# A decoder layer on one core: convolution taps of six pairs moved from accumulating DMAs to VectorE, and a snapshot of begun products taken earlier

## The chip, the cores and the metric

The kernel runs on one core of a Trainium2 chip. The metric is the device time in microseconds (us), lower is better. TensorE is called PE, VectorE DVE, ScalarE ACT, GpSimd POOL and SyncE SP, as the profile does.

## What is computed

One layer of a network on 512 tokens of width 2048, batch 1, in float32: an input projection, a gated convolution beside dilated attention, an output projection, LayerNorm, and then the part around the change, a gated MLP of width 5632 with a causal convolution of width 3 between its two projections, and a second LayerNorm.

```python
def _causal_conv3(x, w):
    xp = jnp.pad(x, ((0, 0), (2, 0), (0, 0)))
    return w[0] * xp[:, :-2] + w[1] * xp[:, 1:-1] + w[2] * xp[:, 2:]

def _conv_ffn(h, w_up, conv_w, conv_b, w_down):
    up = _causal_conv3(h @ w_up, conv_w) + conv_b
    a, g = jnp.split(up, 2, axis=-1)
    return (jax.nn.silu(g) * a) @ w_down

def reference(x, ...):
    mix = _token_mixer(x, w_in, conv_w, w_out, rel_bias)     # conv mixer and attention
    x = _layernorm(ALPHA * x + mix, ln1_g, ln1_b)
    ffn = _conv_ffn(x, w_up, ffn_conv_w, ffn_conv_b, w_down)
    return _layernorm(ALPHA * x + ffn, ln2_g, ln2_b)
```

## The kernel before

**Order of the work.** Four stages follow each other: the input projection (48 pairs of column tiles, 0 to about 965 us), attention with the start of the output projection, the up projection (44 pairs, about 1265 to 2125 us), and the down projection. Each engine runs its own instructions strictly in the order in which the program issues them; nothing is scheduled by a planner. Work that must wait is put off with `later(n, fn)`: a list that `tick()` counts down by one after every product. Loads of weights go through SP's queue, stores and the accumulating transfers through POOL's.

**Pairs and products.** The two projections are computed by a Strassen-Winograd scheme: a pair of column tiles takes seven products, numbered 1 to 7, instead of eight. Each product accumulates into one half of a PSUM bank ("m" with the regions x1 and x2, "n" with x3 and x4). A later product adds to the same region, so between the two ACT must copy the region out; this copy is a snapshot (`snap`, L476, and L455 in wide pairs). Products 1, 5, 6 and 7 have one.

**Splits.** Weights are float32 and are multiplied in two parts. For each product DVE first forms a combination of the weight blocks if it needs one (T1 to T4, lines 207, 209, 211), ACT rounds it to `whi` (L221), DVE subtracts (`wlo`, L224). A ring of four such parts is filled ahead of PE: after a product is freed, the split of the product four places on is issued. So on ACT the snapshots stand between the `whi` of later products.

**Start of a projection.** While the inputs of later products are still being formed, `run_pre` begins one plain pair (pair 0) and products 1 and 2 of five further pairs (pairs 1 to 5). These five are finished afterwards by `run_pairs` with the remaining products `REST = [5, 6, 3, 7, 4]`; pairs from 6 on run all seven (`MAIN = [1, 5, 2, 6, 3, 7, 4]`) in `run_wide`. In a rest pair the order of the accumulations is: product 6 and then 7 go into x1, where product 1 is; product 3 goes into x3, where product 5 is. So snapshot 1 must be done before product 6 starts, snapshot 5 before product 3 and snapshot 6 before product 7.

**After a pair.** `combine` on DVE (L675) adds the banks and the snapshots to the pair's output `o`, first for bank m, then for n; n is combined after the first product of the next pair. Then `done3` makes the convolution and the gate: ACT writes the last tap and the bias to `cv` (L1130); for each of the other two taps ACT scales `o` (L1136) and a DMA on POOL's queue adds the shifted result to `cv` (L1137); seven ticks after `done3` for pairs 0 to 5, nine for later ones, ACT applies the silu to one half of `cv` (L1142), and one tick on DVE multiplies the halves (L1147) and a DMA stores them (`act_d`). For the last pair, 43, the taps are made on DVE instead (`taps`, two SCALAR_TENSOR_TENSOR of 128x511 and 128x510 for each half, L701), with no accumulating DMA:

```python
        def gate():
            if last:
                taps(cv[:, 1], o[:, 1], fw_t[:, j + FT])
            nc.scalar.activation(cv[:, 1], cv[:, 1], AF.Silu)
```

In the input projection `done1` uses the same `taps` for its pairs of kind c (after a multiplication on DVE, L710, and two scaled copies on ACT, L713), and a multiplication L717 closes a pair of kind b.

## Time and profile before

| | us |
|---|---|
| runs before, median of 3 (lowest, highest) | 2617.13 (2614.83, 2621.01) |
| the profiled execution's own time | 2616.42 |
| its span, first to last instruction | 2614.5 |
| PE, DVE, ACT, POOL busy in the span | 2572.5, 2109.6, 1317.6, 228.1 |

The profiled execution took 2616.42 us, 1.9 us more than its span. A busy PE is not yet a PE at its peak: the clock that the chip grants to TensorE is at full speed (2.4 GHz) or at half (1.2 GHz). In the rows "idle before <-releaser" is how long the engine waited before an instruction and what ended that wait.

### The profile page before, as it was taken

What the parts mean: (1) busy time and instruction counts of PE and PEld (TensorE: products, weight loads), DVE (VectorE), ACT (ScalarE), POOL (GpSimd) and SP (SyncE); (2) the same over time, 40 slices, a digit from 0 to 9 for tenths busy, and PEclk for the clock granted to TensorE, in tenths of its full rate; (3) what the DMA queues carried; (4) which work ended last, traced back from release to release, by engine and by line L of the source; (5) the groups of instructions that cost most, each with busy time, mean ns of one, the idle gap of its engine ahead of it and who ended that gap; (6) DMA issues with size and microseconds to landing.
All of it is one profiled execution on the core that took longest, in us unless ns stands there. A gap on an engine that the chain in (4) does not pass through costs nothing.

```text
span 2614.5 us, 36642 instructions
## 1 busy us (share of the span) xinstructions
PE 2572.5 (98%) x14634; PEld 2257.9 (86%) x14634; DVE 2109.6 (81%) x2553; ACT 1317.6 (50%) x1789; POOL 228.1 (9%) x301
## 2 busy tenths in 40 slices
PE   9999999999999999999989999999999999999997
PEld 8988888888888888888987888888888888888886
DVE  7889899899898887656868899889888866765557
ACT  5444444444444454435656676676676653222220
POOL 0000100000000012221011111111111110000000
PEclk9999999999999999999999999999999999999999
DMA  7333534334334367653566666667666683434331
GB/s 261 137 107 136 178 133 151 121 135 148 121 138 144 121 238 263 222 182 113 177 182 169 165 176 182 165 178 180 165 180 178 165 257 142 153 125 161 113 113 65
DMA packets 93610, 421.13 MB, mean 161 GB/s; under 512 B 11296, under 2 KB 37184, under 8 KB 58752
## 3 DMA queue, kind: packets, MB, share of 16 engines
q1 hardware_dynamic: 51968, 313.57, 34.9%
q0 software_dynamic: 41472, 105.22, 16.2%
q8 instruction: 115, 1.88, 0.3%
q14 instruction: 55, 0.45, 0.1%
HBM read 328.61 MB, written 48.84 MB: 144 GB/s over the span
## 4 chain that ended last, share of the span: by engine, by line
PE 88%; DVE 4%; DMA 3%; issue 2%; ACT 2%; SPq 0%; POOL 0%; DVEq 0%; ACTq 0%; POOLq 0%
PE bk L355 38%; PE bk L358 20%; PE bk L524 8%; PE bk L523 8%; PE bk L525 8%; PE bk L382 1%; PE bk L379 1%; PE bk L378 1%; DMA cv<-t 1%; DVE wlo L224 1%; ACT whi L221 1%; PE bk L856 1%; DMA cv<-o 1%; DMA ar<-act_d 1%; PE bk L802 1%
## 5 line engine op out<-in xcount | busy, mean ns | idle before, releaser
L221 ACT ACTIVATE whi<-raw 128x1024 fp32r<-128x1024 f32 x754 | 791.0, 1056 | 834.4 <-PE bk L525 223.5
L224 DVE TENSOR_TENSOR wlo<-raw,whi 128x1024 fp32r<-128x1024 f32 x754 | 919.7, 1221 | 170.4 <-ACT whi L221 157.7
L355 PE MATMUL bk<-S,whi 128*128 128x512 f32 x2560 | 643.2, 393 | 6.3 <-ACT z L455 6.1
L355 PEld LDWEIGHTS bk<-S,whi 128*128 128x128 f32 x2560 | 461.4, 189 | 89.6 <-ACT z L455 6.5
L355 PE MATMUL bk<-A,whi 128*128 128x512 f32 x1920 | 481.4, 393 | 0.0
L355 PEld LDWEIGHTS bk<-A,whi 128*128 128x128 f32 x1920 | 345.6, 189 | 63.3 <-issue 0.9
L358 PEld LDWEIGHTS bk<-S,wlo 128*128 128x128 f32 x2560 | 350.1, 191 | 25.1
L358 PE MATMUL bk<-S,wlo 128*128 128x256 f32 x2560 | 357.7, 283 | 0.0
L358 PEld LDWEIGHTS bk<-A,wlo 128*128 128x128 f32 x1920 | 261.9, 190 | 18.7
L358 PE MATMUL bk<-A,wlo 128*128 128x256 f32 x1920 | 267.7, 282 | 0.0
L524 PE MATMUL bk<-wlo,A 128*128 128x512 f32 x480 | 187.0, 389 | 1.6 <-DVE wlo L224 1.6
L525 PE MATMUL bk<-whi,A 128*128 128x512 f32 x480 | 186.7, 389 | 0.0
L523 PE MATMUL bk<-whi,A 128*128 128x512 f32 x480 | 186.7, 389 | 0.0
L436 DVE TENSOR_TENSOR z<-bk,z 128x512 f32<-128x512 f32 x152 | 104.2, 686 | 64.6 <-ACT z L433 64.6
L455 ACT ACTIVATE s<-bk 128x512 f32<-128x512 f32 x126 | 75.2, 597 | 129.6 <-PE bk L358 129.5
L1004 DVE TENSOR_TENSOR zz<-zz,bk 128x512 f32<-128x512 f32 x144 | 97.7, 687 | 32.9 <-PE bk L525 32.4
L455 ACT ACTIVATE z<-bk 128x512 f32<-128x512 f32 x114 | 67.3, 590 | 91.0 <-PE bk L358 91.0
L209 DVE TENSOR_TENSOR raw<-raw,raw 128x1024 f32<-128x1024 f32 x90 | 109.7, 1219 | 0.4
L211 DVE TENSOR_TENSOR raw<-raw,raw 128x1024 f32<-128x1024 f32 x90 | 109.8, 1220 | 0.0
L211 DVE TENSOR_TENSOR raw<-raw 128x1024 f32<-128x1024 f32 x90 | 109.8, 1220 | 0.0
L207 DVE TENSOR_TENSOR raw<-raw 128x1024 f32<-128x1024 f32 x90 | 109.7, 1218 | 0.0
L524 PEld LDWEIGHTS bk<-wlo,A 128*128 128x128 f32 x480 | 90.1, 188 | 20.8 <-DVE wlo L224 2.2
(216 smaller groups left out, 3406.8 us busy)
## 6 DMA issues: line engine op xcount, KB each, us to landing
raw<-in_w_in_dram SPq DMA_DIRECT2D x97, 1024.0 KB, 5.0
raw<-in_w_up_dram SPq DMA_DIRECT2D x89, 1024.0 KB, 7.5
raw<-in_w_down_dram SPq DMA_DIRECT2D x44, 1024.0 KB, 4.9
cv<-t POOLq DMA_DIRECT2D x43, 511.0 KB, 9.4
cv<-o POOLq DMA_DIRECT2D x43, 510.0 KB, 5.0
qkv_d<-o POOLq DMA_DIRECT2D x36, 512.0 KB, 3.1
raw<-in_w_out_dram SPq DMA_DIRECT2D x16, 1024.0 KB, 7.0
act_d<-cv POOLq DMA_DIRECT2D x44, 256.0 KB, 9.3
```

Source lines behind the costliest of these rows:

```text
L207: nc.vector.tensor_sub(b["T"], v[0], v[1])
L209: nc.vector.tensor_sub(b["T"], v[0], b["T"])
L211: nc.vector.tensor_sub(v[0], v[0], b["T"])
L221: nc.scalar.activation(self.hi, self.src, AF.Copy)
L224: nc.vector.tensor_sub(self.lo, self.src, self.hi.bitcast(F32))
L355: mm(ps, op.hi[:, w], X[xn].both(k), start=first and k == 0, stop=False, skip_group_check=True)
L358: mm(ps[:, 256:], op.lo[:, w], X[xn][0][:, k], start=False, stop=last and k == 7, skip_group_check=True)
L436: nc.vector.tensor_add(u, pairb[p][reg], u)
L455: nc.scalar.activation(sn[q], pairb[p][PROD[q][2]], AF.Copy)
L523: mm(banks[n], yh[:, tt], op.hi[:, w], start=first and i == 0, stop=False)
L524: mm(banks[n], yh[:, tt], op.lo[:, w], start=False, stop=False)
L525: mm(banks[n], yl[:, tt], op.hi[:, w], start=False, stop=last and i == 1)
```

## The change

For pairs 0 to 5 of the up projection the taps are made on DVE as for pair 43 (`last` holds for `j < 6`), with the silu one tick after the pair's combination and the product of the halves two ticks after it. And snapshot 1 of each rest pair, in both projections, is no longer taken when the pair begins: `prepare(p + 1)` takes it after product 3 of the pair before (for pair 1: after the second product of the plain pair), together with the allocation of the pair's two snapshot tiles.

```diff
-TAPS, TAPSPRE = 9, 7
+TAPS = 9
...
+    early = {}
+
+    def prepare(p, stile):
+        sn = early[p] = {b: stile(b).rearrange("p (a t) -> p a t", a=2) for b in "mn"}
+        b, i = SNAP[1]
+        nc.scalar.activation(sn[b][:, i], region(p, PROD[1][2]), AF.Copy)
+
-    def run_plain(pl, X, otile, done, hook):
+    def run_plain(pl, X, otile, done, hook, stile):
...
                 op = product(p, q, X, not _banks(q) & set().union(*map(_banks, seq[i + 1:])))
+                if i == 1 and p + 1 in [r for r, s, _ in pl if s == REST]:
+                    prepare(p + 1, stile)
...
-            sn = {b: stile(b).rearrange("p (a t) -> p a t", a=2) for b in "mn"}
+            sn = early.pop(p)
...
-            if 1 not in seq:
-                snap(1)
...
                 if q in SNAP:
                     snap(q)
+                if q == 3 and p + 1 in [r for r, s, _ in pl if s == REST]:
+                    prepare(p + 1, stile)
...
-        o, cv, last = fh(o), fh(cvtile()), j == FT - 1
+        o, cv, last = fh(o), fh(cvtile()), j == FT - 1 or j < sum(PRE3)
...
-        n = TAPSPRE if j < sum(PRE3) else TAPS
-        later(n, gate)
-        later(n + 1, mul)
+        later(TAPS, gate)
+        later(TAPS + 1, mul)
```

Lines move by 8 to 10: in the rows of the change L404 is `prepare`'s snapshot, L486 the other snapshots, L1140 the last tap with its bias, L1152 the silu, L711 the taps, L685 the combination, L1157 the product of the halves.

ACT in the up projection, from the silu of pair 0 to the last snapshot of pair 2 and the first of pair 3, before (bk_1624 is bank m of pair 2, bk_1719 its bank n, bk_1628 bank m of pair 3, where the second and third of its snapshots read):

```order
L1142 ACT_TABLE_LOAD
L1142 ACTIVATE cv_11835<-cv_11835 128x512
L1136 ACTIVATE t_12070<-o_11966,fw_t 128x512 x2
L476 ACTIVATE z_11969<-bk_1624_11166 128x256
L221 ACTIVATE whi_12099<-raw_11868 128x1024
L1136 ACTIVATE o_11966<-o_11966,fw_t 128x512 x2
L221 ACTIVATE whi_12133<-raw_11866 128x1024
L476 ACTIVATE z_12139<-bk_1628_11197 128x256
L476 ACTIVATE z_12139<-bk_1737_12142 128x256
L221 ACTIVATE whi_12169<-raw_11868 128x1024
L476 ACTIVATE z_12140<-bk_1628_11197 128x256
```

The same stretch of ACT in the change, from the last tap of pair 1 on:

```order
L1140 ACTIVATE cv_12003<-o_11969,fw_t 128x512 x2
L486 ACTIVATE z_11900<-bk_1624_11166 128x256
L221 ACTIVATE whi_12032<-raw_11868 128x1024
L1152 ACTIVATE cv_12003<-cv_12003 128x512
L404 ACTIVATE z_12067<-bk_1628_11197 128x256
L221 ACTIVATE whi_12072<-raw_11868 128x1024
L486 ACTIVATE z_11900<-bk_1624_11166 128x256
L221 ACTIVATE whi_12104<-raw_11870 128x1024
L221 ACTIVATE whi_12133<-raw_11868 128x1024
L486 ACTIVATE z_12067<-bk_1735_12139 128x256
L221 ACTIVATE whi_12166<-raw_11870 128x1024
```

The silu (there of pair 0, here of pair 1) no longer stands ahead of scaled taps; the copies L1136 are gone; snapshot 1 of pair 3 (from bk_1628) stands three products ahead of snapshot 5 (from bk_1735); the last tap L1140 stands between the `whi` and snapshot 6 of pair 2.

DVE over one rest pair of the up projection (raw is a weight block, wlo the low half of a split), before:

```order
L207 TENSOR_TENSOR raw_11866<-raw_11866 128x1024
L224 TENSOR_TENSOR wlo_11999<-raw_11671,whi_11998 128x1024
L224 TENSOR_TENSOR wlo_12031<-raw_11866,whi_12030 128x1024
L209 TENSOR_TENSOR raw_11866<-raw_11868,raw_11866 128x1024
L224 TENSOR_TENSOR wlo_12067<-raw_11866,whi_12066 128x1024
L1147 TENSOR_TENSOR cv_11835<-cv_11835 128x512
L211 TENSOR_TENSOR raw_11866<-raw_11866 128x1024
L224 TENSOR_TENSOR wlo_12100<-raw_11868,whi_12099 128x1024
L675 TENSOR_TENSOR o_12137<-bk_1624_11166,z_11968 128x2x256
L211 TENSOR_TENSOR raw_11868<-raw_11868,raw_11866 128x1024
L224 TENSOR_TENSOR wlo_12134<-raw_11866,whi_12133 128x1024
L675 TENSOR_TENSOR o_12137<-bk_1719_11971,z_11969 128x512
```

DVE over the same stretch in the change:

```order
L207 TENSOR_TENSOR raw_11868<-raw_11868 128x1024
L224 TENSOR_TENSOR wlo_11999<-raw_11671,whi_11998 128x1024
L711 SCALAR_TENSOR_TENSOR cv_12003<-o_11969,fw_t,cv_12003 128x511
L711 SCALAR_TENSOR_TENSOR cv_12003<-o_11969,fw_t,cv_12003 128x510
L224 TENSOR_TENSOR wlo_12033<-raw_11868,whi_12032 128x1024
L209 TENSOR_TENSOR raw_11868<-raw_11870,raw_11868 128x1024
L711 SCALAR_TENSOR_TENSOR cv_12003<-o_11969,fw_t,cv_12003 128x511
L711 SCALAR_TENSOR_TENSOR cv_12003<-o_11969,fw_t,cv_12003 128x510
L1157 TENSOR_TENSOR cv_12003<-cv_12003 128x512
L224 TENSOR_TENSOR wlo_12073<-raw_11868,whi_12072 128x1024
L211 TENSOR_TENSOR raw_11868<-raw_11868 128x1024
L224 TENSOR_TENSOR wlo_12105<-raw_11870,whi_12104 128x1024
```

Four taps now stand in each pair, two behind the split that follows T1 (L207) and two behind T2 (L209), and the multiplication of the halves, which was that of an earlier pair, follows its own taps. The last rows of the fence before, with the combinations L675, stand in the change behind those shown.

ACT at the start of the rest pairs of the input projection (sm and sn are snapshot tiles, bk_31_152 is bank m of pair 1 and bk_103_782 its bank n), before:

```order
L533 ACTIVATE S_94_663<-o_657 128x2x256
L221 ACTIVATE whi_719<-raw_434 128x1024
L221 ACTIVATE whi_746<-raw_477 128x1024
L221 ACTIVATE whi_775<-raw_434 128x1024
L476 ACTIVATE sm_779<-bk_31_152 128x256
L476 ACTIVATE sm_779<-bk_103_782 128x256
L221 ACTIVATE whi_809<-raw_477 128x1024
L402 ACTIVATE o_813<-bk_53_334 128x256
```

And in the change:

```order
L543 ACTIVATE S_94_663<-o_657 128x2x256
L404 ACTIVATE sm_717<-bk_31_152 128x256
L221 ACTIVATE whi_722<-raw_434 128x1024
L221 ACTIVATE whi_749<-raw_477 128x1024
L221 ACTIVATE whi_778<-raw_434 128x1024
L486 ACTIVATE sm_717<-bk_103_782 128x256
L221 ACTIVATE whi_809<-raw_477 128x1024
L410 ACTIVATE o_813<-bk_53_334 128x256
L410 ACTIVATE o_813<-bk_57_369 128x256
L486 ACTIVATE sn_718<-bk_31_152 128x256
```

Snapshot 1 has moved ahead of three `whi`, snapshot 5 stays behind them. Apart from these moves no engine has other instructions in another order: PE's and SP's sequences are the same, and POOL's loses the twelve accumulating transfers of pairs 0 to 5.

## Rows read from the trace of the kernel before

**Rows 1.** The page's first part: busy time, share of the span and number of instructions of each engine.

```profile
PE 2572.5 (98%) x14634; PEld 2257.9 (86%) x14634; DVE 2109.6 (81%) x2553; ACT 1317.6 (50%) x1789; POOL 228.1 (9%) x301
```

**Rows 2.** The waits of PE over the whole run, those at the rest pairs and behind them: who waited for whom, us in total, times, longest us.

```profile
PE bk L378 <- ACT z L476: 8.4, 3, 3.1
PE bk L355 <- ACT z L455: 6.1, 2, 3.1
PE bk L378 <- ACT sm L476: 3.5, 1, 3.5
```

**Rows 3.** PE in order of time, first matmuls of products: start us, duration us, engine, line, operation, tiles and shapes, count, in brackets the idle time before and its releaser. The first two are product 7 and product 4 of pair 2 of the up projection; then the stalled product 6 of pair 3, and that of pair 4 with the product that follows it; then the stalled product 7 of wide pair 7 and the three products that follow it; the last three rows are product 6 of pair 1 of the input projection, the product after it, and product 7 of pair 2 there.

```profile
1307.99 0.28 PE L378 MATMUL bk<-S,whi 128*128 128x256 f32 x1
1310.87 0.28 PE L378 MATMUL bk<-A,whi 128*128 128x256 f32 x1
...
1319.79 0.39 PE L378 MATMUL bk<-S,whi 128*128 128x256 f32 x1 [3.01 <-ACT z L476]
...
1337.60 0.39 PE L378 MATMUL bk<-S,whi 128*128 128x256 f32 x1 [3.14 <-ACT z L476]
...
1342.07 0.28 PE L378 MATMUL bk<-S,whi 128*128 128x256 f32 x1
...
1407.59 1.22 PE L355 MATMUL bk<-S,whi 128*128 128x512 f32 x2 [3.12 <-ACT z L455]
...
1412.88 0.94 PE L355 MATMUL bk<-A,whi 128*128 128x512 f32 x2
...
1416.00 2.00 PE L355 MATMUL bk<-A,whi 128*128 128x512 f32 x8
...
1418.79 0.63 PE L355 MATMUL bk<-S,whi 128*128 128x512 f32 x2
...
70.07 0.58 PE L378 MATMUL bk<-S,whi 128*128 128x256 f32 x1 [3.50 <-ACT sm L476]
...
75.36 0.37 PE L378 MATMUL bk<-S,whi 128*128 128x256 f32 x1
...
92.70 0.28 PE L378 MATMUL bk<-S,whi 128*128 128x256 f32 x1
```

**Rows 4.** Windows of some us: window and its length, busy us and count of PE, weight loads, DVE, ACT, POOL, then the granted clock (1.00 is 2.4 GHz, 0.50 is 1.2 GHz), the DMA share and GB/s.

```profile
70.00:75.00 5.00, 4.93 (x23) 4.93 (x24) 4.41 (x6) 1.89 (x5) 0.00 (x0) 0.50 0.43 121
1336.00:1342.00 6.00, 4.40 (x24) 4.41 (x25) 6.00 (x7) 2.87 (x5) 1.18 (x1) 0.72 0.92 201
...
1408.00:1414.00 6.00, 6.00 (x20) 5.05 (x20) 5.69 (x7) 3.72 (x5) 0.53 (x1) 0.54 0.96 297
```

**Rows 5.** The first row is the longest entry of the waits of ACT from 1280 to 1420 us, the second that of DVE's waits for the silu there; then ACT in order of time before the stall at 1319.79: the silu with its table load, and two snapshots of pair 3 (columns as in rows 3).

```profile
ACT cv L1142 <- DMA cv<-o: 18.3, 5, 6.6
...
DVE cv L1147 <- ACT cv L1142: 15.8, 5, 6.0
...
1312.94 1.28 ACT L1142 ACT_TABLE_LOAD   x1 [2.61 <-DMA cv<-o]
...
1319.38 0.64 ACT L476 ACTIVATE z<-bk 128x256 f32<-128x256 f32 x2
```

**Rows 6.** DVE in order of time: in the input projection the T1 of a pair, two of its four taps, the multiplication that closes a pair and the T1 of the next pair; in the up projection the T1 of pair 2, and a multiplication of halves of pair 43 behind its silu; last a row of the view of line 701, with the number and the least, median and longest duration in ns of pair 43's taps.

```profile
88.80 1.22 DVE L207 TENSOR_TENSOR raw<-raw 128x1024 f32<-128x1024 f32 x1
...
91.07 1.53 DVE L701 SCALAR_TENSOR_TENSOR o<-o,cw_t,o 128x511 f32<-128x511 f32 x2
...
103.35 1.22 DVE L717 TENSOR_TENSOR o<-o,o 128x1024 f32<-128x1024 f32 x1
104.49 1.22 DVE L207 TENSOR_TENSOR raw<-raw 128x1024 f32<-128x1024 f32 x1
...
1290.61 1.22 DVE L207 TENSOR_TENSOR raw<-raw 128x1024 f32<-128x1024 f32 x1
...
2135.32 0.69 DVE L1147 TENSOR_TENSOR cv<-cv 128x512 f32<-128x512 f32 x1 [3.22 <-ACT cv L1142]
...
L701 DVE SCALAR_TENSOR_TENSOR cv<-o,fw_t,cv x4: 745/751/752, 2130.6 to 2136.7; 128x511 f32<-128x511 f32 x2, 128x510 f32<-128x510 f32 x2
```

**Rows 7.** The links of a chain over two engines in order of time: on DVE the combination of bank n of pair 1 and the T1 behind it; on ACT a snapshot, and the two instructions of the last tap with the start of the next instruction.

```profile
1303.12 0.68 DVE L675 TENSOR_TENSOR o<-bk,z 128x512 f32<-128x512 f32 x1
1303.72 1.22 DVE L207 TENSOR_TENSOR raw<-raw 128x1024 f32<-128x1024 f32 x1
...
1359.13 0.38 ACT L476 ACTIVATE z<-bk 128x256 f32<-128x256 f32 x1 [1.58 <-PE bk L382]
...
1360.36 1.51 ACT L1130 ACTIVATE cv<-o,fw_t 128x512 f32<-128x512 f32 x2
1361.78 1.04 ACT L221 ACTIVATE whi<-raw 128x1024 fp32r<-128x1024 f32 x1
```

**Rows 8.** ACT and DVE in order of time in the input projection: the snapshots 1 and 5 of pair 1, DVE's wait behind the late product 6, and the scaled copies L713 with snapshot 6 of pair 2 behind them.

```profile
69.65 0.64 ACT L476 ACTIVATE sm<-bk 128x256 f32<-128x256 f32 x2
...
76.96 1.23 DVE L224 TENSOR_TENSOR wlo<-raw,whi 128x1024 fp32r<-128x1024 f32 x1 [1.36 <-ACT whi L221]
...
88.91 1.34 ACT L713 ACTIVATE o<-o,cw_t 128x512 f32<-128x512 f32 x2 [0.44 <-DVE o L710]
...
90.16 0.36 ACT L476 ACTIVATE sn<-bk 128x256 f32<-128x256 f32 x1
```

More of the change, by code (lines that the diff above doesn't have):

```diff
@@ L723, in done1 @@
             nc.gpsimd.dma_start(qkv_d[a:a + 2, :, slot, :].rearrange("h p t -> p h t"), o)
-    run_plain(plan1, X, otile1, done1, hook)
+    run_plain(plan1, X, otile1, done1, hook, stile1)
     run_pairs(plan1, X, stile1, otile1, bands1, done1, None, block1)
@@ L1157, in done3 @@
             later(1 + sh, functools.partial(tap, sh))
-        n = TAPSPRE if j < sum(PRE3) else TAPS
-        later(n, gate)
-        later(n + 1, mul)
-    run_plain(plan3, X, otile3, done3, hook)
+        later(TAPS, gate)
+        later(TAPS + 1, mul)
+    run_plain(plan3, X, otile3, done3, hook, stile3)
     def block3(p, o, block, u):
```

## The prediction

> **What bounds the kernel now.** I read the page's first part first. TensorE is busy for 2572.5 us of the span and VectorE for 81% of it [rows 1], so there is little idle time to win on PE, and VectorE is the next busiest engine, not ScalarE. The second view is PE's waits. The three entries in [rows 2] are snapshots of the kind that the change touches: 8.4 us before product 6 of rest pairs 3, 4 and 5, 6.1 us before product 7 of wide pairs 6 and 7, and 3.5 us before product 6 of pair 1 in the input projection. The third view is PE in order of time [rows 3]: each of these stalls is 2 to 3.5 us long and stands once in a pair, so something on ACT comes late once in a pair.
>
> What that is, [rows 5] shows. The silu L1142 waits for the accumulating DMAs into cv, 18.3 us in five waits, the longest 6.6. In pair 0 a table load stands there too: it starts at 1312.94 and lasts 1.28 us. ACT works in order, so everything behind the silu is late: snapshots 1 and 5 of pair 3 start at 1319.38 as a group of two, and product 6, which needs the first of them, starts at 1319.79. VectorE's multiplication waits for the same silu, 15.8 us in five waits. The stall in the input projection has another cause. There snapshot 1 stands behind three `whi`, runs at 69.65 [rows 8], and product 6 starts at 70.07 [rows 3].
>
> A stall costs more than its length. Around it the granted clock is 0.50 in the window from 70, 0.72 in the one from 1336 and 0.54 in the one from 1408 [rows 4], that is, TensorE ran partly at 1.2 GHz behind an idle PE. In [rows 3] a product's pitch at full clock is 1310.87 − 1307.99 = 2.88 us, in wide pairs 1418.79 − 1416.00 = 2.79. The slow ones are 1342.07 − 1337.60 = 4.47 (1.59 too long), 1412.88 − 1407.59 = 5.29 (2.50 too long), 1416.00 − 1412.88 = 3.12 (0.33 too long) and, in the input projection, 75.36 − 70.07 = 5.29 (2.41 too long).
>
> **The change part by part.** *Removed: the accumulating DMAs and the wait for them.* The silu now waits for two taps on VectorE that are issued just ahead of it, and no snapshot stands behind a transfer. That takes away the two up-projection entries, 8.4 + 6.1 = 14.5 us [rows 2], and the clock lost there, 1.59 + 2.50 + 0.33 = 4.42 us [rows 3]. The four scaled copies L1136 of each pair leave ACT too; ACT is busy for half the span [rows 1], so beyond the stalls already counted I put them at nothing.
>
> *Moved: snapshot 1, three products sooner.* In the up projection it covers the same stalls and has no second gain. In the input projection it frees product 6 of pair 1 at once. Product 6 can start 3.5 us sooner, about 66.6, and the clock need not fall; at most that is 3.50 + 2.41 = 5.9 us. But snapshot 5 stays behind the three `whi`. It then runs where the two stood, at 69.65 [rows 8], and with 0.36 for one snapshot it ends at 70.0; product 3, one product of 2.88 behind 66.6 and so due at 69.4, waits about 0.6 us for it. Then a second limit comes: product 7 of pair 2 starts at 92.70 [rows 3], and needs snapshot 6, which runs at 90.16 for 0.36 behind the scaled copies L713, which wait for VectorE's L710 [rows 8]. VectorE itself comes forward only by its wait at 76.96, 1.36 us [rows 8]. So snapshot 6 is done at 90.52 − 1.36 = 89.2 at best, and the stretch gains 92.70 − 89.2 = 3.5 us. I take 3.5. The lower bound is what stays if the clock falls behind the new waits as it did before, 3.5 − 2.4 = 1.1; the upper is 5.9.
>
> *Added: four taps for each rest pair on VectorE.* Two take 1.53 us together in the input projection, one about 751 ns in pair 43 [rows 6]; both rows agree. VectorE's time for a rest pair with such taps stands in the trace: from T1 at 88.80 to T1 at 104.49, 15.69 us [rows 6]. That pair closes with L717 (1.22), the new ones with a multiplication L1147 (0.69) instead, so 15.69 − 1.22 + 0.69 = 15.16 us. PE needs five products of 2.88, 14.40. VectorE thus falls back by 0.76 us in each pair, where it had time to spare before.
>
> What is late then is found along one chain: the combination of bank n → the last tap L1140 (issued at once now, ahead of the snapshot) → snapshot 6 → product 7. VectorE's T1 of pair 2 stands at 1290.61 [rows 6] and is not moved by the change; the T1 of the next pair comes 15.16 later, 1305.77, and the combination before it 0.60 earlier (1303.72 − 1303.12 [rows 7]), 1305.17. Its 0.68, with the hand-over 0.72, then 1.42 for the two last taps (1361.78 − 1360.36) and 0.38 for the snapshot [rows 7], end at 1307.69; product 7 of pair 2 starts at 1307.99 [rows 3]. So pair 2 just has no stall (margin 0.3). Pair 3 then lacks 0.76 − 0.3 = 0.5, and pairs 4 and 5 lack 0.76 each, if the rest of PE's pitch is kept: 0.5 + 0.76 + 0.76 = 2.0 us of new, short stalls. VectorE's own splits I count at nothing: the ring holds four products, 4 × 2.88 = 11.5 us of PE's work, and the drift over four pairs is 3.0. The clock did fall behind stalls of 3 us, but not behind all five of them; I assume that pieces below 0.8 do not move it. The ends of this term are nothing, if VectorE keeps to 14.40, and the 14.9 us of the dearer rival below.
>
> The product of the halves is hidden too if the silu, issued one tick before, ends while VectorE does the split, T2 and two taps (about 1.2 + 1.2 + 1.5 = 3.9 us by [rows 6]). Without that cover it costs a wait like the 3.22 us of pair 43 [rows 6].
>
> *The sum* against the profiled execution's 2616.42, which is 0.7 below the runs' median of 2617.13: 2616.4 − 14.5 − 4.4 − 3.5 + 2.0 = 2596.0 us.
>
> At one place a rule speaks against the edit. VectorE is busy for 81% of the span as a whole and, by 15.16 against 14.40, wholly in these pairs [rows 1, 6]. The Trainium skill, page "Perfetto Trace Analysis", section "Optimizing Scalar/DVE Operations", says that where DVE is saturated it may pay to move work from it to Scalar; this change goes the other way. By that rule the six pairs should lose, which is the second rival; by the rows the excess is 0.76 us a pair, less than the 2 to 3 us a pair that the waits cost. No run so far shows the rule at work here.
>
> **The rivals.** *Better: VectorE keeps up.* The pair takes at most 14.40 and the input projection gives all of its 5.9: 2616.4 − 14.5 − 4.4 − 5.9 = 2591.6. For it speaks that the 15.69 us of [rows 6] hold whatever pauses VectorE had in that pair; against it, that the chain's margin is only 0.3.
>
> *Dearer: VectorE becomes the bound.* The multiplication waits for the silu as in pair 43, 3.22 us in each of four pairs, on an engine with no slack: 2.0 + 4 × 3.22 = 14.9 us of stalls in place of 2.0. That gives 2616.4 − 14.5 − 4.4 − 3.5 + 14.9 = 2608.9, with the clock's 4.4 kept as well 2613.3. For it: ACT has the last tap, a snapshot and a `whi` between combination and silu. Against it: the 3.9 us of cover.
>
> *No change.* ACT still stands in front of the silu, now for VectorE's taps, and the snapshots behind it come as late as before; only the input projection gains, up to its 3.5: 2612.9 to 2616.4. Against it, the snapshot that product 6 needs is now ahead by three products.
>
> *Slower.* The multiplication waits 6.0 us a pair, the longest of [rows 5], and VectorE hands all of it to PE: 2.0 + 4 × 6.0 = 26.0, the clock falls as before, and the time is 2616.4 − 14.5 − 3.5 + 26.0 = 2624.4. It decides from (5.2 + 14.5 + 3.5 − 2.0) / 4 = 5.3 us a pair on. What speaks against it is that the 6.0 came from a silu that itself waited 6.6 for a transfer, which is gone.
>
> **How the numbers follow.** Forecast 2596, with its own range of 2593.6 (the input projection gives 5.9) to 2600.4 (some of the clock's 4.4 stays): 0.68. Better, 0.13; dearer, 0.13; no change, 0.03; slower, 0.03. The predicted time is 2596. The range reaches from 2590.5, a little below the better case, to 2604, where a wait of about half of 3.22 (four times 2.0, or 8 us) stands; past it lie most of the dearer case and the two last ones. A measurement of this kernel cannot tell less than about 0.2% (5.2 us) from no change. Forecast, better and nearly all of the dearer case are faster by more: 0.93; same 0.04, slower 0.03.
>
> **What would show it.** Right: PE's waits for snapshots at product 6 and wide product 7 are gone; in rest pairs 3 to 5 short ones, below 1 us, stand before product 7, with the last tap as what runs on ACT just before; VectorE's T1 comes every 15.2 us; no wait of the silu for a DMA; the granted clock between 1336 and 1414 stays at 1.00; product 7 of pair 2 in the input projection starts near 89.2. Wrong: a wait of VectorE for the silu of over 1 us in each pair, stalls that sum to more than 5 us there, or new stalls in wide pairs 6 and 7.

## The result and the profile after

The changed kernel takes 2595.96 us (median of 4 runs, 2594.98 to 2597.53), the kernel before 2616.61 beside it (4 runs). The ratio is 0.9921, 95% interval 0.9908 to 0.9933: 20.65 us faster. A second measurement with the experiments gave 2598.39 against 2617.53, ratio 0.9928 (0.9916 to 0.9940).

The page's first part and the waits of PE over the whole run, after, to be read beside [rows 1, 2]. In the changed kernel L486 is the snapshot, with tiles z in the up projection and sm and sn in the input projection:

```profile
PE 2566.5 (99%) x14634; PEld 2252.4 (87%) x14634; DVE 2125.2 (82%) x2577; ACT 1304.4 (50%) x1765; POOL 214.0 (8%) x289
...
PE bk L534 <- DVE wlo L224: 1.8, 1, 1.8
...
PE bk L378 <- ACT sn L486: 1.6, 1, 1.6
PE bk L378 <- ACT z L486: 1.6, 3, 0.6
...
PE bk L378 <- ACT sm L486: 0.5, 1, 0.5
```

Of the 18.0 us of [rows 2] the snapshots now cost 3.7, and the entry of the wide pairs (6.1 us, line 355) has gone altogether. VectorE has 24 instructions more, the taps.

PE in order of time, after: in the input projection product 3 of pair 1 and product 7 of pair 2; in the up projection product 7 of pairs 2, 3, 4 and 5, then in wide pair 7 product 7 in its two parts (`whi` L355, `wlo` L358) and the product behind it.

```profile
70.47 0.39 PE L378 MATMUL bk<-S,whi 128*128 128x256 f32 x1 [0.53 <-ACT sm L486]
...
89.64 0.39 PE L378 MATMUL bk<-S,whi 128*128 128x256 f32 x1 [1.64 <-ACT sn L486]
...
1305.03 0.28 PE L378 MATMUL bk<-S,whi 128*128 128x256 f32 x1
...
1320.07 0.39 PE L378 MATMUL bk<-S,whi 128*128 128x256 f32 x1 [0.48 <-ACT z L486]
...
1335.30 0.39 PE L378 MATMUL bk<-S,whi 128*128 128x256 f32 x1 [0.57 <-ACT z L486]
...
1350.53 0.39 PE L378 MATMUL bk<-S,whi 128*128 128x256 f32 x1 [0.58 <-ACT z L486]
...
1389.90 2.00 PE L355 MATMUL bk<-S,whi 128*128 128x512 f32 x8
1391.74 1.12 PE L358 MATMUL bk<-S,wlo 128*128 128x256 f32 x8
1392.69 2.00 PE L355 MATMUL bk<-A,whi 128*128 128x512 f32 x8
```

Set beside [rows 3], product 7 of pair 2 of the input projection comes 92.70 − 89.64 = 3.06 us sooner. This execution had begun the rest pairs 0.5 us later (product 5 of pair 1 starts at 64.02, before at 63.53), so the stretch itself gained 3.5. In the up projection product 7 of pair 2 stands 1307.99 − 1305.03 = 2.96 ahead, product 7 of wide pair 7 1407.59 − 1389.90 = 17.69 ahead, and the product behind it 1412.88 − 1392.69 = 20.19, since no slow clock follows any more. Between product 7 of one rest pair and of the next there are 15.23 us (1335.30 − 1320.07, 1350.53 − 1335.30) where PE's own work is 14.40.

ACT and DVE, after, around the last tap of pair 1 in the up projection: ACT's last tap L1140 with the snapshot 6 behind it and the silu L1152; VectorE's T1, the product of the halves and the T1 of the next pair.

```profile
1303.00 1.52 ACT L1140 ACTIVATE cv<-o,fw_t 128x512 f32<-128x512 f32 x2 [0.62 <-DVE o L685]
1304.43 0.36 ACT L486 ACTIVATE z<-bk 128x256 f32<-128x256 f32 x1
1304.70 1.04 ACT L221 ACTIVATE whi<-raw 128x1024 fp32r<-128x1024 f32 x1
1306.77 0.63 ACT L1152 ACTIVATE cv<-cv 128x512 f32<-128x512 f32 x1 [1.03 <-DVE cv L711]
...
1302.88 1.21 DVE L207 TENSOR_TENSOR raw<-raw 128x1024 f32<-128x1024 f32 x1
...
1310.63 0.69 DVE L1157 TENSOR_TENSOR cv<-cv 128x512 f32<-128x512 f32 x1
...
1318.11 1.22 DVE L207 TENSOR_TENSOR raw<-raw 128x1024 f32<-128x1024 f32 x1
```

From T1 to T1 VectorE takes 1318.11 − 1302.88 = 15.23 us, the same as PE's pitch. The product of the halves has no wait before it; the silu waits 1.03 us for taps, where in [rows 5] it waited for a DMA.

The windows of [rows 4] after, and last 5 us behind the wait of 1.8 us at the start of the down projection (granted clock in the third column from the end):

```profile
70.00:75.00 5.00, 4.53 (x37) 4.54 (x38) 4.40 (x7) 2.35 (x7) 0.00 (x0) 1.00 0.31 95
1336.00:1342.00 6.00, 6.00 (x53) 6.00 (x52) 5.79 (x8) 3.38 (x6) 0.00 (x0) 1.00 0.65 244
...
1408.00:1414.00 6.00, 6.00 (x35) 5.25 (x35) 5.74 (x9) 4.64 (x7) 1.78 (x2) 1.00 0.95 308
...
2140.00:2145.00 5.00, 5.00 (x16) 3.93 (x17) 3.24 (x3) 1.98 (x4) 0.00 (x0) 0.66 0.82 295
```

The clock now stays at 2.4 GHz in the three stretches in which it had fallen. In this execution it fell in another, which the change does not touch: behind a wait of 1.8 us at the start of the down projection. That gave back 1.8 us (20.5 us ahead at the end of the up projection, 2614.5 − 2595.8 = 18.7 at the end of the span).

### The profile page after: what moved, and what is told of

Same layout as the page of the kernel before. It is cut to its first block, busy times and chain, and to the rows that moved or that the text cites. A ratio compares the mean times of both kernels' runs of the same rounds, so it can differ in the third digit from the quotient of the medians.

```text
span 2595.8 us, 36627 instructions
## 1 busy us (share of the span) xinstructions
PE 2566.5 (99%) x14634; PEld 2252.4 (87%) x14634; DVE 2125.2 (82%) x2577; ACT 1304.4 (50%) x1765; POOL 214.0 (8%) x289
## 4 chain that ended last, share of the span: by engine, by line
PE 90%; DVE 4%; ACT 1%; issue 1%; DMA 1%; SPq 0%; DVEq 0%; ACTq 0%
PE bk L355 39%; PE bk L358 20%; PE bk L533 8%; PE bk L535 8%; PE bk L534 8%; DVE wlo L224 1%; PE bk L378 1%; PE bk L379 1%; PE bk L382 1%; PE bk L866 1%; DMA ar<-act_d 1%; PE bk L812 1%; DVE raw L211 1%; PE bk L796 0%; ACT whi L221 0%
## 5 line engine op out<-in xcount | busy, mean ns | idle before, releaser
L355 PE MATMUL bk<-S,whi 128*128 128x512 f32 x2560 | 641.3, 392 | 0.2 <-ACT s L465 0.2
L355 PEld LDWEIGHTS bk<-S,whi 128*128 128x128 f32 x2560 | 460.4, 189 | 82.8 <-ACT s L465 0.4
L355 PE MATMUL bk<-A,whi 128*128 128x512 f32 x1920 | 481.1, 392 | 0.0
L355 PEld LDWEIGHTS bk<-A,whi 128*128 128x128 f32 x1920 | 345.3, 189 | 63.2 <-issue 0.9
L358 PEld LDWEIGHTS bk<-S,wlo 128*128 128x128 f32 x2560 | 349.2, 190 | 24.9
L358 PE MATMUL bk<-S,wlo 128*128 128x256 f32 x2560 | 356.9, 282 | 0.0
L358 PEld LDWEIGHTS bk<-A,wlo 128*128 128x128 f32 x1920 | 261.9, 190 | 18.7
L358 PE MATMUL bk<-A,wlo 128*128 128x256 f32 x1920 | 267.7, 282 | 0.0
L209 DVE TENSOR_TENSOR raw<-raw,raw 128x1024 f32<-128x1024 f32 x90 | 109.8, 1220 | 0.4
L207 DVE TENSOR_TENSOR raw<-raw 128x1024 f32<-128x1024 f32 x90 | 109.6, 1218 | 0.0
```

The source lines that it names most:

```text
L207: nc.vector.tensor_sub(b["T"], v[0], v[1])
L209: nc.vector.tensor_sub(b["T"], v[0], b["T"])
L355: mm(ps, op.hi[:, w], X[xn].both(k), start=first and k == 0, stop=False, skip_group_check=True)
L358: mm(ps[:, 256:], op.lo[:, w], X[xn][0][:, k], start=False, stop=last and k == 7, skip_group_check=True)
```

## The experiments

All runs, each with its median, the median of the kernel before measured beside it, and the ratio with its interval:

| version | us | before | ratio (95%) |
|---|---|---|---|
| taps only | 2599.43 | 2615.27 | 0.9939 (0.9926 to 0.9953) |
| snapshot moved only | 2615.62 | 2615.27 | 0.9998 (0.9989 to 1.0007) |
| input projection as before | 2600.03 | 2615.27 | 0.9943 (0.9928 to 0.9958) |
| last tap one product later | 2597.23 | 2615.27 | 0.9927 (0.9915 to 0.9940) |
| silu without cover | 2607.88 | 2617.36 | 0.9966 (0.9953 to 0.9978) |
| last tap and scaled copies later | 2594.68 | 2617.36 | 0.9914 (0.9900 to 0.9929) |
| taps on VectorE for all pairs | 2632.47 | 2617.36 | 1.0058 (1.0043 to 1.0073) |
| both later, product on GpSimd | 2596.06 | 2617.53 | 0.9922 (0.9910 to 0.9935) |
| both later, five pairs | 2593.52 | 2617.53 | 0.9910 (0.9896 to 0.9923) |
| the change again | 2598.39 | 2617.53 | 0.9928 (0.9916 to 0.9940) |
| both later, four pairs | 2593.23 | 2617.14 | 0.9907 (0.9890 to 0.9923) |

The rest pairs of the input projection begin at 63.53 to 67.33 us in the thirteen profiled executions, up to 3.8 us apart. So single terms of 1 or 2 us are read from distances between products within one trace: from product 5 of pair 2 of the up projection to the third product behind product 7 of wide pair 7, 35 products, it is 119.45 us before and 101.89 in the change. A second trace of the change gives 101.88.

### The two parts apart

**The taps alone.** `prepare` is called where the pair begins:

```diff
-                if i == 1 and p + 1 in [r for r, s, _ in pl if s == REST]:
-                    prepare(p + 1, stile)
...
-                if q == 3 and p + 1 in [r for r, s, _ in pl if s == REST]:
-                    prepare(p + 1, stile)
...
+            prepare(p, stile)
             sn = early.pop(p)
```

> The taps of pairs 0 to 5 stay on VectorE; snapshot 1 is taken when its own rest pair begins, as in the kernel before, in both projections. My account: the input projection loses its 3.5 us again (stall of 3.5 at product 6 of pair 1 and the slow clock behind it). In the up projection snapshot 1 stands behind the rounding of the product three places on, which waits for VectorE; in the trace of the changed kernel that rounding ends 1.1 to 1.5 us behind the start of product 6 of pairs 3 to 5, so product 6 waits 0.6 to 1.5 us in some of these pairs, and the short waits before product 7 shrink by as much; in sum 1.5 us more. Together 5.0 us above the changed kernel: about 2601. Rival 1 (the two parts cover the same stalls in the up projection, so the snapshot's move does nothing there): 2599.5. Rival 2 (the snapshot's move did most of it): above 2606, with product 6 of pairs 3 to 5 waiting 2 to 3 us as before.

Measured: 2599.43. PE's product 6 of pair 1 in the input projection, then product 6 of pairs 3 and 4 in the up projection (L404 is `prepare`'s snapshot):

```profile
70.77 0.58 PE L378 MATMUL bk<-S,whi 128*128 128x256 f32 x1 [3.63 <-ACT sm L404]
...
1318.69 0.39 PE L378 MATMUL bk<-S,whi 128*128 128x256 f32 x1 [0.57 <-ACT z L404]
...
1333.92 0.39 PE L378 MATMUL bk<-S,whi 128*128 128x256 f32 x1 [0.57 <-ACT z L404]
```

The stall of the input projection is back, 3.63 us. In the up projection the waits before product 7 of the change are replaced by waits of the same length before product 6, and the distance over the 35 products is 102.65, only 0.76 above the change. The 0.76 is mostly a fourth wait, of 0.41 us, in pair 2. So there the taps do nearly all of the work, and moving the snapshot is worth less than 1 us beside them. The time is the first rival's (2599.5), but by its account the move does nothing there: 0.76 lies halfway between that and my 1.5.

**The snapshot alone.** The taps stay accumulating DMAs:

```diff
-        o, cv, last = fh(o), fh(cvtile()), j == FT - 1 or j < sum(PRE3)
+        o, cv, last = fh(o), fh(cvtile()), j == FT - 1
...
-        later(TAPS, gate)
-        later(TAPS + 1, mul)
+        n = 7 if j < sum(PRE3) else TAPS
+        later(n, gate)
+        later(n + 1, mul)
```

> The accumulating DMAs stay for pairs 0 to 5, with the silu seven ticks on; only snapshot 1 is taken three products sooner. My account: the input projection keeps its 3.5 us; in the up projection product 6 of pairs 3 to 5 no longer waits, but snapshot 5 still stands behind the silu that waits for a DMA and is needed one product (2.9 us) later, so about 0.4 us a pair is left; the stalls at product 7 of the wide pairs 6 and 7 (6.1 us and 2.8 us of clock) stay. 2616.6 - 3.5 - 7.3 - 1.6 = about 2604. Rival 1 (it is the wait for the DMA alone that counts, wherever the snapshot stands): 2613. Rival 2 (the snapshot's place alone would have done): 2597 or less, without stalls in the wide pairs.

Measured: 2615.62, no gain (0.9998). The longest entry of ACT's waits from 1280 to 1420 us; ACT in order of time, a silu of that stretch, the scaled copies L1146 behind it and snapshot 5 of pair 4; and PE's product 3 of pair 4:

```profile
ACT cv L1152 <- DMA cv<-o: 21.7, 5, 7.7
...
1331.15 0.63 ACT L1152 ACTIVATE cv<-cv 128x512 f32<-128x512 f32 x1 [5.05 <-DMA cv<-o]
1331.69 1.32 ACT L1146 ACTIVATE t<-o,fw_t 128x512 f32<-128x512 f32 x2
...
1334.12 1.32 ACT L1146 ACTIVATE o<-o,fw_t 128x512 f32<-128x512 f32 x2
...
1336.30 0.36 ACT L486 ACTIVATE z<-bk 128x256 f32<-128x256 f32 x1
...
1336.71 0.58 PE L378 MATMUL bk<-S,whi 128*128 128x256 f32 x1 [4.10 <-ACT z L486]
```

Product 6 no longer waits, as I had said, but product 3, the next one, does: 4.1 us in pair 4, more than the 3.14 that went. My account left out that PE now arrives earlier (it waits 0.61 us in pair 3 instead of 3.01) while the transfer does not come forward as far: the silu's waits grow from 18.3 to 21.7 us, and snapshot 5 stands behind it. Over the 35 products the distance is 120.95, 1.5 more than before, and that eats half of the 3.3 us that the input projection gained in this trace; the rest is not to be told from the scatter of the runs. So moving one snapshot does not help while the silu ahead of the others waits for the DMA. From the silu to snapshot 5 it is 5.15 us, and about half of it is the two groups of scaled copies, which the taps on VectorE take away too; the wait and the copies were not tested apart in these pairs.

**The input projection's snapshot undone.**

```diff
-                if i == 1 and p + 1 in [r for r, s, _ in pl if s == REST]:
+                if i == 1 and pl is not plan1 and p + 1 in [r for r, s, _ in pl if s == REST]:
...
-                if q == 3 and p + 1 in [r for r, s, _ in pl if s == REST]:
+                if q == 3 and pl is not plan1 and p + 1 in [r for r, s, _ in pl if s == REST]:
...
+            if pl is plan1:
+                prepare(p, stile)
             sn = early.pop(p)
```

> The change, but in the input projection snapshot 1 is taken when its rest pair begins, as before. My account: the stall of 3.5 us at product 6 of pair 1 comes back with 2.4 us of slow clock, and what it gives back at product 7 of pair 2 as in the kernel before: 3.5 us above the changed kernel, 2599.5, and nothing else differs. Rival (the early part of the run shifts later transfers and splits, and the 3.5 us are made good on the way): 2596.

Measured: 2600.03, 4.1 above the change's first median and 1.6 above its second, which were not taken beside it: the sign is as forecast, the size is not settled by this run. Its profiled execution is a special one: it began the rest pairs 3.2 us later than the change's (67.25 against 64.02), and product 6 waited only 1.06 us. The 35 products of the up projection take the same 101.89 as in the change, so in this trace the two projections do not touch each other. Over 42 products from product 5 of pair 1 on, the kernel before and the taps alone take 125.61 and 125.85 us, the change 122.16, which is 3.5 and 3.7 less. But this distance depends on when the rest pairs begin: six traces with the input projection of the change give 120.90 to 122.62, and this run, with its late start and the snapshot as before, 120.81. In medians taken side by side, this run is 2.8 us above the next one (2597.23), which has the input projection of the change and an up projection 0.8 shorter; that leaves 2.0 for the term.

### The new waits

**The last tap one product later.**

```diff
         if last:
-            start()
-            later(1, gate)
-            later(2, mul)
+            late = int(j < FT - 1)
+            later(late, start) if late else start()
+            later(late + 1, gate)
+            later(late + 2, mul)
```

> The change, but the last tap with its bias on ScalarE, the taps, the silu and the product of the halves of pairs 0 to 5 are each issued one product later, so that the last tap stands behind snapshot 6 of the next pair. My account: the waits of 0.5 to 0.6 us before product 7 of pairs 3 to 5 come from the last tap that stands ahead of snapshot 6 and itself waits for VectorE's combination; they go, with the slower first matmuls behind them 2.1 us, and the drift of VectorE (0.8 us a pair) is held by the four splits of the ring: 2593.9. Rival (VectorE's 15.2 us a pair bound the rest pairs as such): the waits turn up in front of another product, same time, 2596.

Measured: 2597.23, in the same range as the change. PE's waits for snapshots from 1270 to 1430 us, in order of time: product 3 of pair 5, and product 7 of wide pair 6.

```profile
1346.41 0.39 PE L378 MATMUL bk<-S,whi 128*128 128x256 f32 x1 [0.54 <-ACT z L486]
...
1369.63 2.12 PE L355 MATMUL bk<-S,whi 128*128 128x512 f32 x8 [0.36 <-ACT z L465]
```

Both accounts were half right. The three waits before product 7 are gone, so they came by the last tap. But two others appear, and the 35 products take 101.09, only 0.8 less than the change instead of 2.1. VectorE has no wait from 1290 to 1365 us, and in the change it had none from 1288 to 1349 either: its pitch of 15.2 for 14.4 is the limit in both, and the last tap is only the shortest way by which it reaches PE. With that way longer, it shows later and not at a split, which is four products ahead of PE, but at a snapshot: ACT takes snapshots between the roundings `whi`, and these wait for VectorE's combinations. ACT just before the wait at 1346.41, a rounding and snapshot 5 behind it:

```profile
1345.03 1.06 ACT L221 ACTIVATE whi<-raw 128x1024 fp32r<-128x1024 f32 x1 [2.66 <-DVE raw L211]
1346.00 0.36 ACT L486 ACTIVATE z<-bk 128x256 f32<-128x256 f32 x1
```

**VectorE's cover taken away.** All four taps stand ahead of the silu, the product directly behind it:

```diff
         def gate():
+            if last and j < FT - 1:
+                taps(cv[:, 0], o[:, 0], fw_t[:, j])
             if last:
                 taps(cv[:, 1], o[:, 1], fw_t[:, j + FT])
...
-            if last:
+            if j == FT - 1:
                 taps(cv[:, 0], o[:, 0], fw_t[:, j])
...
             later(1, gate)
-            later(2, mul)
+            later(2 if j == FT - 1 else 1, mul)
```

> The change, but in pairs 0 to 5 all four taps stand ahead of the silu and the product of the halves directly behind it, so that VectorE has no work of its own while ScalarE does the silu. This prices the rival in which VectorE waits for the silu. The changed kernel's silu ends about 0.7 us after the taps it waits for, and 2.1 us where a table load stands before it, so VectorE waits 0.7 to 1 us in each pair. My account: VectorE hands this on to PE through the last tap and snapshot 6, about 0.8 us in each of pairs 2 to 5, 3 us in all: 2599. Rival 1 (the ring of four splits holds it): 2596. Rival 2 (the wait is the 3.2 us of pair 43 in each pair): 2606 to 2609.

Measured: 2607.88. DVE's waits from 1290 to 1365 us, two of DVE's instructions in pair 3, and PE's waits at product 3 and 7 of that pair:

```profile
DVE cv L1159 <- ACT cv L1154: 5.1, 5, 2.0
DVE wlo L224 <- ACT whi L221: 4.7, 4, 1.2
...
1316.70 1.23 DVE L224 TENSOR_TENSOR wlo<-raw,whi 128x1024 fp32r<-128x1024 f32 x1 [1.19 <-ACT whi L221]
...
1329.59 0.69 DVE L1159 TENSOR_TENSOR cv<-cv 128x512 f32<-128x512 f32 x1 [0.76 <-ACT cv L1154]
...
1320.54 0.38 PE L378 MATMUL bk<-S,whi 128*128 128x256 f32 x1 [0.39 <-ACT z L486]
...
1325.54 0.39 PE L378 MATMUL bk<-S,whi 128*128 128x256 f32 x1 [1.87 <-ACT z L486]
```

VectorE loses 5.1 + 4.7 = 9.8 us, and the 35 products take 112.49, 10.6 more than in the change: what VectorE waits, PE waits. The time is that of my second rival, but not by its mechanism. The wait for the silu is 0.76 us as I had worked out (2.0 where the table load is). What I had not seen is the second entry: in the change two taps stand between T2 and the split that needs ACT's rounding of T2, and cover that round trip; without them it costs 1.19 us in each pair.

**Taps on VectorE for all pairs.**

```diff
-        o, cv, last = fh(o), fh(cvtile()), j == FT - 1 or j < sum(PRE3)
+        o, cv, last = fh(o), fh(cvtile()), True
```

> The change, with the taps on VectorE for all 44 pairs instead of the first six and the last; no accumulating transfer is left. It tests whether work on VectorE is free where VectorE is nearly full. In the wide pairs of the changed kernel VectorE is busy for 17.45 of 19.53 us; the taps add 2.9 to 3.0, and 1.6 us of its idle time is a wait for PE inside the pair. My account: the demand of 20.4 us exceeds PE's 19.53 by 0.8 to 0.9 us in each of 37 pairs; the ring's slack of about 5 us is used up and then PE waits: 2596 + 37 x 0.85 - 5 = about 2622. Rival 1 (there is room: VectorE's wait for PE is filled and PE keeps its pace): 2596. Rival 2 (fewer transfers beside the weights and an emptier ScalarE make it faster): below 2594.

Measured: 2632.47, slower than the kernel before (1.0058). A window as long as ten wide pairs of the kernel before (busy us of PE, weight loads, DVE, ACT, POOL), PE's longest entry of waits over the whole run, and one product in each of two successive pairs:

```profile
1500.00:1695.30 195.30, 188.57 (x1069) 164.46 (x1068) 191.91 (x229) 105.85 (x135) 4.86 (x9) 1.00 0.31 110
...
PE bk L355 <- ACT z L465: 26.5, 36, 0.8
...
1616.81 2.11 PE L355 MATMUL bk<-S,whi 128*128 128x512 f32 x8 [0.75 <-ACT z L465]
...
1637.37 2.11 PE L355 MATMUL bk<-S,whi 128*128 128x512 f32 x8 [0.74 <-ACT z L465]
```

VectorE is busy for 191.91 of 195.30 us, and PE waits about once in each wide pair, 36 times in all, for a snapshot. A pair takes 1637.37 − 1616.81 = 20.56 us instead of 7 × 2.79 = 19.53, 1.03 more, 38 us over 37 pairs, of which 2632.47 − 2596 = 36 show in the time; I had estimated 0.85 and some 5 us that the ring would hold. The rule on a saturated VectorE that the prediction weighed (the Trainium skill, "Perfetto Trace Analysis", "Optimizing Scalar/DVE Operations") agrees with this run, where no wait is bought off with the taps; in the first six pairs the stalls that went were larger than the price.

### Versions that go further

**Last tap and scaled copies later.** In `done1` of the input projection, beside the edit of the last tap:

```diff
-            for f in range(2):
-                nc.scalar.activation(cc[:, f], o[:, f], AF.Copy, scale=cw_t[:, a + f, 2:3])
-                later(1 + f, functools.partial(taps, cc[:, f], o[:, f], cw_t[:, a + f]))
+            late = int(p < sum(PRE1))
+            def scale():
+                for f in range(2):
+                    nc.scalar.activation(cc[:, f], o[:, f], AF.Copy, scale=cw_t[:, a + f, 2:3])
+            later(1, scale) if late else scale()
+            for f in range(2):
+                later(late + 1 + f, functools.partial(taps, cc[:, f], o[:, f], cw_t[:, a + f]))
```

> The run before this one with the later last tap, and in the input projection the two scaled copies on ScalarE of pairs 0 to 5 (and the taps behind them) one product later too, so that snapshot 6 of pair 2 no longer stands behind them. My account: the wait of 1.6 us before product 7 of pair 2 goes as well, with 0.2 us of slower matmuls: 2593.9 - 1.8 = 2592.1. Rival (the next wait takes its place, a split or snapshot of pair 3 that comes late): 2593.9.

Measured: 2594.68. The wait of 1.64 before product 7 of pair 2 does not appear in its trace; the 42 products of the input projection take 120.04 instead of 122.16, those of the up projection 101.08.

**The product of the halves on GpSimd**, in that version:

```diff
-            nc.vector.tensor_mul(cv[:, 0], cv[:, 0], cv[:, 1])
+            eng = nc.gpsimd if last and j < FT - 1 else nc.vector
+            eng.tensor_mul(cv[:, 0], cv[:, 0], cv[:, 1])
```

> The version with both moves (last tap and scaled copies one product later), and the product of the halves of pairs 0 to 5 on GpSimd instead of VectorE. In that version VectorE has no idle time in the rest pairs and PE still waits 0.5 us in pair 5 and 0.4 us in wide pair 6. My account: these two waits are VectorE's rate (about 15.2 us for 14.4 of PE); 0.6 us less for VectorE in each pair brings it to about 14.6, the drift over five pairs falls from 4 to 1 us, the ring holds it, and both waits go with the slower first matmuls behind them: 1.2 us less. Rival 1 (the waits are an order of instructions on ScalarE and not VectorE's rate): unchanged. Rival 2 (GpSimd works beside VectorE at VectorE's cost): taps and splits beside the GpSimd product get longer and the waits grow.

Measured: 2596.06. GpSimd's product of pair 3, and VectorE's split beside it:

```profile
1344.01 2.15 POOL L1164 TENSOR_TENSOR cv<-cv 128x512 f32<-128x512 f32 x1 [12.64 <-ACT whi L221]
...
1344.91 2.32 DVE L224 TENSOR_TENSOR wlo<-raw,whi 128x1024 fp32r<-128x1024 f32 x1
```

The second rival: the split beside it takes 2.32 us instead of 1.22, so VectorE loses 1.1 to save 0.6, and the 35 products take 102.44 instead of 101.08.

The Trainium skill, "Perfetto Trace Analysis", "Optimizing Scalar/DVE Operations", says that work moved between GpSimd and VectorE might not help, because they share a read port to SBUF. The two rows agree that it did not help; that the port is the reason they do not show.

**Taps on VectorE for five pairs, then four**, in the version with both moves:

```diff
-        o, cv, last = fh(o), fh(cvtile()), j == FT - 1 or j < sum(PRE3)
+        o, cv, last = fh(o), fh(cvtile()), j == FT - 1 or j < sum(PRE3) - 1
```

> The version with both moves, with the taps on VectorE for pairs 0 to 4 only; pair 5, whose taps fall into the first wide pair, uses the accumulating DMAs again, with the silu nine products on as in all later pairs. My account: the wait of 0.4 us in wide pair 6 goes (3.0 us less for VectorE there), and with nine products the silu of pair 5 no longer waits for its transfer, so product 7 of wide pair 7 does not stall: 0.5 us less than the version with both moves. Rival (the silu of pair 5 waits for its transfer with nine products as with seven): product 7 of wide pair 7 stalls by up to 3 us, 2 to 5 us more.

> The changed kernel itself once more, beside the two versions on the same chip, so that differences of 1 to 2 us can be read within one call. 2596, as before; the versions with both moves should lie 1.5 to 3 us below it. In its trace the slow clock behind the wait at the start of the down projection (0.66 in the first profile) may be there or not; if it is a matter of chance the span differs by about 1.8 us from 2595.8.

> The version with both moves and the taps on VectorE for pairs 0 to 3 only; pairs 4 and 5 use the accumulating DMAs with the silu nine products on. My account: the taps of pair 4 fell into rest pair 5, where VectorE was late for snapshot 5 before product 3 (0.5 us and 0.2 us of slower matmuls); without them this last wait of the rest pairs goes: 0.7 us less in the trace than with five pairs, about 2593. Rival (nine products on is too soon for pair 4, whose transfer runs while the rest pairs load weights faster than the wide ones): the silu waits for the DMA again, and the snapshots of wide pair 6 or 7 behind it stall PE by 1 to 3 us: 2594 to 2596.

Measured: 2593.52 with five pairs and 2598.39 for the change beside it, and 2593.23 with four (`- 2`). PE's one remaining wait in the rest pairs, with five and with four, and the first 5 us of the down projection in the change's second trace:

```profile
1343.69 0.39 PE L378 MATMUL bk<-S,whi 128*128 128x256 f32 x1 [0.53 <-ACT z L486]
```

```profile
1345.10 0.39 PE L378 MATMUL bk<-S,whi 128*128 128x256 f32 x1 [0.54 <-ACT z L486]
```

```profile
2141.00:2146.00 5.00, 4.92 (x21) 4.05 (x22) 3.49 (x4) 2.23 (x4) 0.00 (x0) 1.00 0.79 274
```

With five pairs the wait in wide pair 6 is gone and no stall comes in pair 7: the 35 products take 100.28. With four they take 100.29, and the wait in pair 5 is still there: the taps of pair 4 are issued behind product 3 of pair 5 and were not its cause, so that expectation was wrong. In the trace with four pairs ACT has no wait for a DMA from 1280 to 1420 us, although pairs 4 and 5 use the accumulating transfers again: nine products are enough there. Whether the silu nine products on would have done for all six pairs, with the transfers kept and no work added to VectorE, was not run; it is the rival of this change that stays open. The clock at the start of the down projection is 1.00 in the change's second trace, with a wait of 2.04 us before it, and 0.66 in the first with 1.82: from the last product of the up projection to the end of the span the first takes 499.16 us and the second 497.82, so 1.3 of the 1.8 us lost there come and go. Beside the change the version with five pairs is 4.9 us faster, where 1.5 to 3 had been expected.

## Why the prediction was right, step by step

- **The waits that go, 14.5 us, and their clock, 4.4 us.** Right, both: neither is left in the trace after. The distance of the up projection fell by 119.45 − 101.89 = 17.56 where the prediction has 14.5 + 4.4 − 2.0 = 16.9. Of the 0.7 more, 0.4 are the new waits, 1.6 instead of 2.0, and 0.3 a term left out: a stall costs PE 0.16 us beyond the idle time of its row (a wait of 0.48 made the pitch 3.52 instead of 2.88), and five stalls became three. That the silu behind its transfer and not the snapshot's place was the cause is shown by the two parts apart, taps alone 102.65 and snapshot alone 120.95. How much of it was the transfer and how much the scaled copies was not tested; with nine products between, pairs 4 and 5 had both and no stall.
- **The snapshot's move "covers the same stalls" in the up projection.** Nearly right: beside the taps it is worth 0.8 us there, where the prediction has nothing.
- **The input projection, 3.5 us.** The path was right: the 0.6 before product 3 (0.53), and the limit by snapshot 6 behind the scaled copies, 89.64, or 89.15 with the 0.49 taken off by which this execution began later, where I had 89.2. Moving those copies took away the wait there and gave 2.1 more in the trace, which confirms the limit. The size is 3.5 between these two traces. But medians taken side by side leave 2.0, with runs that scatter by 2 to 3 us, and in the trace that began late the stall at product 6 was 1.06 instead of 3.50; so 3.5 is not shown for other executions.
- **VectorE's 15.16 us a pair and the new waits, 2.0 us.** 15.23 and 1.6 in waits, 2.1 in PE's pitch up to the three products 7 (3.52, 3.61 and 3.62 for 2.88). Size and path were right: VectorE's drift reaches PE over the last tap and snapshot 6. The sentence that the splits cost nothing was right too. What was wrong is the step that I built on it for the run with the later last tap, that the ring would hold the drift once that path is longer: that gave 0.8 of the 2.1, for other snapshots feel VectorE's rate next.
- **The cover of the silu.** Right: no wait before the product of the halves. Its price without cover, 3.22, came from a wrong reading. The multiplication with that wait in [rows 6] is not of pair 43 but of pair 42, which has accumulating DMAs; its silu, the second in the rows below, is behind four copies (L1185) of the down projection. Pair 43's own multiplication, the last row, follows its taps without a wait:

```profile
2132.19 0.63 ACT L1142 ACTIVATE cv<-cv 128x512 f32<-128x512 f32 x1
2132.72 2.04 ACT L1185 ACTIVATE zz<-bk 128x512 f32<-128x512 f32 x4
2134.63 0.65 ACT L1142 ACTIVATE cv<-cv 128x512 f32<-128x512 f32 x1
...
2137.49 0.69 DVE L1147 TENSOR_TENSOR cv<-cv 128x512 f32<-128x512 f32 x1
```

Without cover the wait is 0.76 us a pair; the 1.19 us of the round trip behind T2 brought the time of the dearer rival about by chance.
- **The sum.** 2596.0 against 2595.96. The agreement to 0.1 us is luck: the same kernel gave 2598.39 in another measurement, and terms of 0.5 to 1.8 us (the slow matmuls, the clock at the start of the down projection, the start of the run) were not in the sum.

## What to carry to other kernels

Look behind a waiting instruction on its engine: here the silu's wait for a transfer was paid by snapshots that had nothing to do with it, and moving one of them only made the next one wait. Work may be moved onto an engine that is nearly full where the stall it removes is larger than that engine's excess, and no further: here 0.8 us a pair was well spent in six pairs, and 1.0 a pair lost 38 us over the others. Four or five pairs did no worse than six. To find where a full engine will hurt, follow the shortest chain from it to PE, not the deepest buffer.

## What the runs showed of the hardware

A GpSimd product of 128x512 float32 took 2.05 to 2.15 us in five pairs and 1.29 in the sixth, where VectorE takes 0.69, and VectorE's 128x1024 subtraction beside it took 2.32 instead of 1.22. TensorE's clock fell to 1.2 GHz behind a wait of 1.8 us in one execution of the changed kernel and not behind one of 2.04 us at the same place in another; over the thirteen traces of all versions it fell there in six, behind waits of 1.82 to 2.04 us, and not in seven, behind waits of 1.27 to 2.06; behind the short waits of 0.5 to 0.6 us in the rest pairs it stayed at 2.4 GHz (1.00 in the window from 1336).
